# Gated values to DRAM, and a down projection by seven products of block sums behind the last block

## The chip, the core and the metric

One core of a Trainium2 chip runs one inference step of a one-layer decoder. The metric is the device time of that step in microseconds (us). The core has five engines that run beside each other and meet at semaphores: TensorE (PE, matmuls and weight loads), VectorE (DVE), ScalarE (ACT), GpSimd (POOL) and SyncE (SP), whose queue issues nearly all DMAs. The 16 DMA engines move the data that SP's queue names.

## The reference, cut to what matters

Everything is float32. Before the part that changes there are a combined input projection, dilated attention, a spatial gate and an output projection; they stay as they are. What changes is this part:

```python
def _swiglu(x, g, w_gate, w_up, w_down):
    h = _rmsnorm(x, g)
    return (jax.nn.silu(h @ w_gate) * (h @ w_up)) @ w_down
...
    x = x + jnp.concatenate([att, u * gate], axis=-1) @ w_out
    x = x + _swiglu(x, norm2_g, w_gate, w_up, w_down)
...
y_prompt = _rmsnorm(xp, final_g)
```

There are 2048 prompt tokens (16 tiles of 128 rows) and 32 sample tokens, 1024 model columns and 2816 hidden columns (22 slices of 128, called f below).

## The kernel before

Float32 matmuls are made of three passes each. An operand is split into a rounded high half (ACT copies it into the rounded type) and the rest, the low half (a subtraction on POOL or DVE), and a product is high by high, high by low, low by high.

The 16 token tiles go through the second half of the layer in three blocks: 6 tiles, 6 tiles, and 4 tiles with the sample rows. In each block the output projection and the second norm come first. Then a loop runs over the 22 slices f. In it the two products with `w_gate` and `w_up` are not made as eight block products but as seven (q = 0 to 6, function `product`): sums of blocks of the tokens and of the weights are multiplied, and the seven results are added up by DVE. Each of the seven is 12 matmuls whose moving side is 64 columns for each tile, 384 wide in a block of 6 tiles and 272 wide in the last one. The weight sums of a slice are made once, in the first block (`sums`, on POOL), are kept in DRAM (`ab_d`, 7 x 256 KB a slice) and are read back in the other two blocks (`load_source`). In the first block `gained` multiplies the raw weight quarters with the second norm's gain, kept in `g2c`, before sums are made of them. `high` and `low_half` split an operand into an `op` tile; `STAGES`, `prepare` and `ahead_of` say at which of the seven products of the slice ahead each of these steps stands.

`hidden` multiplies the gate with the up value and splits the result at once into the high and low half (`hw`). After every second slice, `down_unit` multiplies the two slices' halves with the split rows of `w_down` (`dw`, split on POOL) and DVE adds each 128 x 512 result to the tile's accumulator `acc` in SBUF (line 1763). So the down projection is plain: 16 tiles x 22 slices x 2 halves of the columns x 3 passes, 2112 matmuls of 512 columns, spread over the loops. Behind a block's last slice, `first_downs` and `down_unit` do the last pair, and `final_a`, `final_b` and `final_store` scale by the final norm and store `yp`. In the last block `last_rows` does this.

The order of the work is the order of the Python code; `later(n, fn)` puts a step n ticks ahead, and each product or unit calls `tick()`. All buffers come from pools with few copies: a step that needs a buffer waits until its last reader is done. SP's queue is in order, so that one DMA that waits holds up those behind it. The caches are copied from DRAM to DRAM in 128 pieces of 512 KB (112 whole ones of 512 KB and 16 of 504 KB), one at each `roll(1)`; `roll(len(pieces))` at the end issues what is left, which is nothing.

## Time and profile before

| what | value |
|---|---|
| median of 3 runs | 2527.84 us (2526.73 to 2529.05) |
| profiled execution | 2529.23 us, of which 2527.4 us is the span from the first to the last instruction |
| mean granted TensorE clock | 0.990 |
| PE, DVE, ACT, POOL busy | 2451.9, 1427.4, 1221.2, 1376.7 us |
| DMA | 480.00 MB moved, 190 GB/s on average |

The page gives for each engine its busy time. The share of a stage is read from a table of stretches (start:end in us), which gives for each engine the busy time, the granted clock, the mean share of the 16 DMA engines and the GB/s that they moved. In this execution the loops over f run from about 1030 to 1440 us (first block), 1600 to 2060 us (second) and 2165 to 2500 us (last).

### The profile page before, as it was taken

What the parts mean: (1) busy time and instruction counts of PE and PEld (TensorE: products, weight loads), DVE (VectorE), ACT (ScalarE), POOL (GpSimd) and SP (SyncE); (2) the same over time, 40 slices, a digit from 0 to 9 for tenths busy, and PEclk for the clock granted to TensorE, in tenths of its full rate; (3) what the DMA queues carried; (4) which work ended last, traced back from release to release, by engine and by line L of the source; (5) the groups of instructions that cost most, each with busy time, mean ns of one, the idle gap of its engine ahead of it and who ended that gap; (6) DMA issues with size and microseconds to landing.
All of it is one profiled execution on the core that took longest, in us unless ns stands there. A gap on an engine that the chain in (4) does not pass through costs nothing.

```text
span 2527.4 us, 38918 instructions
## 1 busy us (share of the span) xinstructions
PE 2451.9 (97%) x13598; PEld 2172.8 (86%) x13598; DVE 1427.4 (56%) x2768; ACT 1221.2 (48%) x2578; POOL 1376.7 (54%) x1078
## 2 busy tenths in 40 slices
PE   9999999999999899999999999999999999999997
PEld 7787777778888878999999988999999988999997
DVE  4378785347888866444444475444444466444445
ACT  6414344446877747545545446332323336444333
POOL 1245643233667657767767644653644534766664
PEclk9999999999999999999999999999999999999999
DMA  8863844887687674645646463663544643755553
GB/s 278 247 194 102 296 140 139 251 267 236 203 236 231 170 206 151 211 159 164 200 138 196 162 203 106 215 206 129 202 169 153 213 148 125 258 194 189 194 193 121
DMA packets 313585, 480.00 MB, mean 190 GB/s; under 512 B 25889, under 2 KB 178882, under 8 KB 307502
## 3 DMA queue, kind: packets, MB, share of 16 engines
q1 hardware_dynamic: 308428, 469.00, 57.6%
q10 hardware_dynamic: 4962, 8.51, 1.1%
q8 instruction: 108, 1.77, 0.3%
q14 instruction: 87, 0.71, 0.1%
HBM read 381.72 MB, written 165.83 MB: 217 GB/s over the span
## 4 chain that ended last, share of the span: by engine, by line
PE 57%; POOL 6%; issue 4%; DVE 4%; DMA 2%; ACT 2%; SPq 1%; DVEq 0%; ACTq 0%; POOLq 0%
PE ps_o L1761 18%; PE ps_m L1686 11%; PE ps_m L1684 11%; PE ps_m L1685 11%; POOL o L1108 1%; POOL ob L1110 1%; POOL ob L1106 1%; DMA pair<-f_d 1%; PE ps_o L1434 1%; PE ps_o L1433 1%; PE ps_o L1435 1%; DMA cat_d<-ob 1%; POOL qo L887 1%; DVE pl L944 1%; POOL op L1625 1%
## 5 line engine op out<-in xcount | busy, mean ns | idle before, releaser
L1625 POOL TENSOR_TENSOR op<-fr,op 128x512 fp32r<-128x512 f32 x393 | 499.3, 1300 | 279.4 <-ACT op L1621 267.5
L1686 PE MATMUL ps_m<-xh,op 128*128 128x384 f32 (+5 forms) x1932 | 610.2, 316 | 0.1
L1684 PE MATMUL ps_m<-xh,op 128*128 128x384 f32 (+5 forms) x1932 | 610.1, 316 | 0.0
L1685 PE MATMUL ps_m<-xl,op 128*128 128x384 f32 (+5 forms) x1932 | 609.1, 315 | 0.0
L1761 PE MATMUL ps_o<-dw,hw 128*128 128x512 f32 x2028 | 478.7, 391 | 3.7 <-DVE acc L1763 3.7
L1761 PEld LDWEIGHTS ps_o<-dw,hw 128*128 128x128 f32 x2028 | 377.9, 188 | 82.7 <-DVE acc L1763 7.0
L1763 DVE TENSOR_TENSOR acc<-acc,ps_o 128x512 f32<-128x512 f32 (+1 forms) x360 | 246.6, 687 | 220.4 <-PE ps_o L1761 220.4
L1684 PEld LDWEIGHTS ps_m<-xh,op 128*128 128x128 f32 x1932 | 363.8, 188 | 4.0
L1685 PEld LDWEIGHTS ps_m<-xl,op 128*128 128x128 f32 x1932 | 363.6, 188 | 3.5
L1686 PEld LDWEIGHTS ps_m<-xh,op 128*128 128x128 f32 x1932 | 363.5, 188 | 0.8 <-POOL op L1625 0.8
L1731 ACT ACTIVATE ps_t<-zn 128x384 f32<-128x384 f32 (+2 forms) x132 | 60.0, 454 | 457.1 <-DVE zn L1714 344.0
L1621 ACT ACTIVATE op<-fr 128x512 fp32r<-128x512 f32 x396 | 235.2, 623 | 20.1 <-DMA fr<-ab_d 17.2
L138 POOL TENSOR_TENSOR dw<-fd,dw 128x1024 fp32r<-128x1024 f32 x65 | 156.3, 2405 | 120.7 <-ACT dw L135 120.0
L323 PE MATMUL ps_s<-wh,xh 128*128 128x512 f32 x480 | 195.8, 408 | 6.1 <-ACT xh L135 6.0
L324 PE MATMUL ps_s<-wl,xh 128*128 128x512 f32 x480 | 190.7, 397 | 0.0
L325 PE MATMUL ps_s<-wh,xl 128*128 128x512 f32 x480 | 190.5, 397 | 0.0
L1741 ACT ACTIVATE hw<-ps_t 128x384 fp32r<-128x384 f32 (+2 forms) x132 | 57.7, 444 | 176.6 <-DVE ps_t L1737 175.6
L1625 POOL TENSOR_TENSOR op<-pair,op 128x512 fp32r<-128x512 f32 x63 | 81.2, 1295 | 98.8 <-ACT op L1621 94.6
L323 PEld LDWEIGHTS ps_s<-wh,xh 128*128 128x128 f32 x480 | 91.9, 191 | 35.1 <-issue 7.3
L325 PEld LDWEIGHTS ps_s<-wh,xl 128*128 128x128 f32 x480 | 91.7, 191 | 20.3 <-DVE xl L138 0.3
L324 PEld LDWEIGHTS ps_s<-wl,xh 128*128 128x128 f32 x480 | 92.0, 192 | 17.7 <-DVE wl L226 0.5
L1696 DVE TENSOR_TENSOR raw<-zn,ps_m 128x384 f32<-128x384 f32 (+1 forms) x63 | 32.5, 515 | 123.6 <-PE ps_m L1686 69.1
(503 smaller groups left out, 4801.4 us busy)
## 6 DMA issues: line engine op xcount, KB each, us to landing
fr<-ab_d SPq DMA_DIRECT2D x308, 256.0 KB
fd<-in_w_down_dram SPq DMA_DIRECT2D x66, 512.0 KB
out_ks_dram<-in_cache_k_dram SPq DMA_DIRECT2D x56, 512.0 KB
out_vs_dram<-in_cache_v_dram SPq DMA_DIRECT2D x56, 512.0 KB
ab_d<-fr SPq DMA_DIRECT2D x88, 256.0 KB
raw<-in_w_in_dram SPq DMA_DIRECT2D x72, 256.0 KB
qk_d<-pair SPq DMA_DIRECT2D x64, 256.0 KB
ab_d<-pair SPq DMA_DIRECT2D x63, 256.0 KB
```

The lines of the kernel that those rows point to most:

```text
L138: (eng_lo or pool).tensor_sub(lo, src, hi.bitcast(F32))
L323: pe.matmul(o[j], xh[:, k, :], wh, start=(k == 0), stop=False)
L324: pe.matmul(o[j], xh[:, k, :], wl, start=False, stop=False)
L325: pe.matmul(o[j], xl[:, k, :], wh, start=False, stop=(k == KD - 1))
L1621: act.activation(ops[f, j][0], ab[f][j], AF.Copy)
L1625: (pool if f or j else dve).tensor_sub(lo_, ab[f][j], hi.bitcast(F32))
L1684: pe.matmul(out, wh[:, ks], xh[:, :, k], start=(k == 0), stop=False)
L1685: pe.matmul(out, wh[:, ks], xl[:, :, k], start=False, stop=False)
L1686: pe.matmul(out, wl[:, ks], xh[:, :, k], start=False, stop=(k == 3))
L1731: act.activation(g, c, AF.Silu)
L1761: pe.matmul(ps[0:nr], l_, r_[:, cs], start=(z == 0 and y == 0), stop=(z == FC - 1 and y == len(pairs) - 1))
L1763: dve.tensor_add(B.acc[i][0:nr, cs], B.acc[i][0:nr, cs], ps[0:nr])
```

## The change

Slices 0 to 19 (ten pairs, `NJ = 10`) lose their down projection inside the loops. `hidden` writes the product unsplit into an `hr` tile, sorted into even and odd token tiles, and one DMA for each slice and block stores it to `h_d`. `x1_store` stores the rows after the output projection, with the last pair's share added (slices 20 and 21 are still projected as before), to `x1_d`, in the place where the final norm stood. The sample rows keep the old way.

Behind the last block `second_part` opens a pool `p2` over the loop's buffers and runs `Down`. It takes two halves of the tokens (hv, 1024 rows each, four pairs of an even and an odd tile), and in each seven products of block sums (s = 0 to 6), each a sum over the ten pairs j. So there are 140 steps n, of 12 matmuls of 512 columns each. The blocks are the even and the odd tiles (rows), the two slices of a pair (inner side) and the two halves of the columns of `w_down`. The sums run on DVE and POOL (`Down.sums`); those of `w_down` are made in the first half, stored to `t_d` and read again. The results of a product stay in four PSUM banks over ten steps and go to the accumulators in 4 additions (`evict`); some banks are added to twice and go on summing. Loads are issued six steps ahead, sums and splits three. 46 of the cache pieces are issued between the steps (n % 3 == 0); the loops issue 21 and 42.

The gain of the second norm is now multiplied into the token rows, in one DVE instruction with the norm's scale (`norm2_scale`), so `gained` and the tables for it are gone. `w_gate` and `w_up` come sorted by slice, so that a quarter is one contiguous load, and three of the seven sources are read from the input itself instead of a copy. In the first block sums move from POOL to DVE; in the last block the splits of `w_down` and two of the seven low halves do so.

```diff
-    EVEN_STAGES = ((), ((both_halves, 0), (keep, 3)), ...
+    STAGES = (((sums, 4), (sums, 3), (high, 0)), ((sums, 1), (keep, 4), (keep, 1), (low_half, 0), (high, 1)), ...
...
     def norm2_scale(B, i, r):
-        act.activation(B.xn[i][:n], B.acc[i][:n], AF.Copy, scale=r)
+        dve.scalar_tensor_tensor(B.xn[i][:n], B.acc[i][:n], r, gain[0][:n], op0=OP.mult, op1=OP.mult)
...
+                if fn is low_half and B.last and j in (1, 4):
+                    fn(f, j, dve)
...
+            if f < 2 * NJ and b == B.nt:
+                c0 = B.b0 * 64
+                sync.dma_start(h_d[f].rearrange("q p t -> p q t")[:, :, c0:c0 + B.nt * 64], B.h[f % FC][0])
...
+    def x1_store(B, i, nb):
+        t0 = (B.b0 + i) * P
+        sync.dma_start(x1_d[t0:t0 + P, :], B.acc[i])
...
+    EVICTS = ((0, 0), (0, 0), (0, 1), (1, 1), (1, 1), (0, 1), (1, 0))
+    NS = 7 * NJ
+    TAIL = 3
...
+        def fr(self):
+            return self.p2.tile([P, 512], F32, name="fr2", tag="fr2", bufs=10)
...
+        def load(self, n):
+            hv, s, j = self.at(n)
+            for key, y, q in (((("a11", 0, 0),), (("a21", 0, 1), ("a12", 1, 0)), (("a22", 1, 1),)) + ((),) * 4)[s]:
+                self.a[key, j] = t_ = self.p2.tile([P, 512], F32, name=key, tag=key, bufs=NJ)
+                sync.dma_start(t_, h_d[2 * j + y, q, :, hv * 512:(hv + 1) * 512])
+            if hv == 0 and s == 0:
+                w = [self.b(j, 0, 0), self.b(j, 0, 1), self.b(j, 1, 1, raw_tile)]
+            elif hv == 0 and s == 2:
+                w = [self.t(j, 2), self.b(j, 0, 0)]
...
+        def sums(self, n):
+            if hv == 0 and s == 0:
+                dve.tensor_sub(w[2], w[2], w[1])
+                dve.tensor_sub(w[1], w[1], w[0])
+                sync.dma_start(t_d[j, 2], w[2])
+                sync.dma_start(t_d[j, 0], w[1])
+            elif hv == 0 and s == 2:
+                pool.tensor_add(w[0], w[0], w[1])
+                sync.dma_start(t_d[j, 1], w[0])
...
+            elif s == 2:
+                self.src[n] = x = zn_tile()
+                dve.tensor_sub(x, a22, a21)
+                dve.tensor_add(a11, a11, x)
...
+        def split(self, n):
+            self.ops[n] = (hh, hl), (wh, wl) = op_tile(), op_tile()
+            h, w = self.src.pop(n), self.w.pop(n)[0]
+            act.activation(wh, w, AF.Copy)
+            act.activation(hh, h, AF.Copy)
+            pool.tensor_sub(wl, w, wh.bitcast(F32))
+            dve.tensor_sub(hl, h, hh.bitcast(F32))
...
+        def run(self):
+            for n in range(2 * NS - TAIL):
+                tick()
+                self.sums(n + 3)
+                self.split(n + 3)
+                self.load(n + 6)
...
+                if n % 3 == 0:
+                    roll(1)
+                self.mats(n)
+                if n >= NJ and j < 4:
+                    self.evict(phv, ps_, j, self.prev)
...
-            if f + 1 < NF and q in (1, 3, 5)[:(1, 3, 3 if f < 2 else 2)[bi]]:
+            if f + 1 < NF and q in (1, 4)[:(1, 2, 0)[bi]]:
                 roll(1)
...
         for n, u in enumerate(units):
             for q in range(7):
                 one(u, q)
-                if u["f"] % 2 == 0 and u["f"] > 0 and 3 <= q < 6:
-                    downs_of((B.h[0], B.h[1]), *((0, 2), (2, 4), (4, 9))[q - 3])
+                if B.last and u["f"] % 2 == 0 and u["f"] > 0 and q == 4:
+                    down_unit(B, len(rows) - 1, (B.h[0], B.h[1]))
```

On PE, in the second block between the products q = 3 and q = 4 of an even slice, before (`xh`, `xl` are the tokens' halves, `op` the weights', `dw` and `hw` the halves of `w_down` and of the gated values; x6 is six in a row):

```order
L1685 MATMUL ps_m_18920<-xl_15488,op 128x384
L1686 MATMUL ps_m_18920<-xh_15487,op 128x384
L1761 MATMUL ps_o_18941<-dw,hw 128x512 x6
L1761 MATMUL ps_o_18949<-dw,hw 128x512 x6
L1761 MATMUL ps_o_18957<-dw,hw 128x512 x6
L1761 MATMUL ps_o_18965<-dw,hw 128x512 x6
L1684 MATMUL ps_m_18973<-xh_15487,op 128x384
```

Twelve down matmuls for each of two tiles stood there. Now the next product follows at once:

```order
L1664 MATMUL ps_m_17071<-xh_13994,op 128x384
L1665 MATMUL ps_m_17071<-xl_13995,op 128x384
L1666 MATMUL ps_m_17071<-xh_13994,op 128x384
L1664 MATMUL ps_m_17092<-xh_13994,op 128x384
L1665 MATMUL ps_m_17092<-xl_13995,op 128x384
```

No down matmul stands between them. And on PE behind the last block, at the start of the new part:

```order
L1754 MATMUL ps_o_22591<-dw,hw 128x512 x6
L1754 MATMUL ps_o_22599<-dw,hw 128x512 x6
L1897 MATMUL ps_m_22628<-op 128x512
L1898 MATMUL ps_m_22628<-op 128x512
L1899 MATMUL ps_m_22628<-op 128x512
```

The down matmuls of 20 slices leave the loops and come back behind the last block as lines 1897 to 1899; over the whole program PE has 240 matmuls of 512 columns fewer (4688 for 4928) and the same number of every other width.

On SP, the head of the new part's loads (`a` is a block of `h_d`, `fr` and `raw` blocks of `w_down`, `t_d` the stored sums, `ac` and `x_d` the rows of `x1_d`):

```order
L1855 DMA t_d<-raw 128x512
L1856 DMA t_d<-fr_22587 128x512
L1834 DMA a_22686<-h_d 128x512
L1820 DMA fr_22688<-in_w_down_dram 128x512
L1820 DMA fr_22690<-in_w_down_dram 128x512
L1820 DMA raw<-in_w_down_dram 128x512
L1907 DMA ac<-x_d 128x1024 x2
L1782 DMA x_d<-acc_18410 128x1024
```

Stores of sums, loads of a later step and the traffic of the token rows share one queue, in this order; nothing of it stood there before. SP's end, before:

```order
L1330 DMA out_vs_dram<-in_cache_v_dram 16x8064
L1664 DMA fd<-in_w_down_dram 128x1024
L1808 DMA out_yp_dram<-acc_21019 128x1024
L1808 DMA out_yp_dram<-acc_21068 128x1024
L1808 DMA out_yp_dram<-acc_21121 128x1024
L1808 DMA out_yp_dram<-acc_21169 128x1024
L1810 DMA out_ys_dram<-acc_20969 32x1024
```

The last cache piece stood ahead of the last stores of rows. SP's end now:

```order
L1970 DMA out_yp_dram<-ac 128x512 x8
L1333 DMA out_vs_dram<-in_cache_v_dram 16x8192 x2
L1333 DMA out_vs_dram<-in_cache_v_dram 16x8064
L1333 DMA out_vs_dram<-in_cache_v_dram 16x8192 x7
L1333 DMA out_vs_dram<-in_cache_v_dram 16x8064
L1333 DMA out_vs_dram<-in_cache_v_dram 16x8192 x7
L1333 DMA out_vs_dram<-in_cache_v_dram 16x8064
```

Now 19 pieces of the caches (2 + 1 + 7 + 1 + 7 + 1) stand behind the very last store of rows.

On DVE, two steps of the first half's third product (hv 0, s = 2), a stretch that did not exist before:

```order
L1868 TENSOR_TENSOR zn<-a_23041,a_22751 128x512
L1869 TENSOR_TENSOR a_22453<-a_22453,zn 128x512
L1883 TENSOR_TENSOR op<-zn,op 128x512
L1868 TENSOR_TENSOR zn<-a_23066,a_22782 128x512
L1869 TENSOR_TENSOR a_22461<-a_22461,zn 128x512
L1883 TENSOR_TENSOR op<-zn,op 128x512
```

Three DVE instructions belong to a step. On POOL, the last step of the product ahead of it and two steps of this one:

```order
L1882 TENSOR_TENSOR op<-fr_23019,op 128x512
L1858 TENSOR_TENSOR fr_23043<-fr_23043,fr_23045 128x512
L1882 TENSOR_TENSOR op<-fr_23043,op 128x512
L1858 TENSOR_TENSOR fr_23068<-fr_23068,fr_23070 128x512
L1882 TENSOR_TENSOR op<-fr_23068,op 128x512
```

Each step there has three DVE and two POOL instructions whose operands all lie in SBUF; in the other products it has one to three on DVE and one on POOL.

More of the change, by code (lines that the diff above doesn't have):

```diff
@@ L1836, in last_rows, with second_part @@
+    def second_part(B, h):
+        m = len(B.rows) - 1
+        left.close()
+        gain.append(row_tile("final_g"))
+        d = Down(left.enter_context(tc.tile_pool(name="p2", bufs=1, reuse_waits="tile")))
+        for n in range(3):
+            d.load(n)
         first_downs(B, 0, 1, h)
-        squares(0, sa, 0)
-        squares(1, sa, 1)
+        d.sums(0)
+        d.split(0)
+        d.load(3)
         down_unit(B, m, h)
-        roots(sa, va, ra, 0, 2)
-        tick()
-        y = square_tile()
@@ L1856, in last_rows @@
-        squares(3, sb, 2)
-        scaled_row(2, rb_[:, 0:1])
-        roots(sb, vb, rb_, 2, 3)
-        newton(rb_[:, 2:3], vb[:, 2:3])
-        scaled_row(3, rb_[:, 2:3])
-        scaled_row(m, rb_[:, 1:2])
+        d.sums(1)
+        d.split(1)
+        d.load(4)
+        down_unit(B, 2, h)
+        d.sums(2)
+        d.split(2)
+        d.load(5)
+        down_unit(B, 3, h)
+        sync.dma_start(gain[1], dap(A["final_g"], 0, [[0, P], [1, D]]))
+        for i in range(m):
+            later(1 + i, x1_store, B, i, None)
@@ L1864, in hymba_step, with sample_final @@
+        def sample_final():
+            y = square_tile()
+            x = B.acc[m]
+            act.activation(y[0:SR], x[SR:2 * SR], AF.Copy)
+            dve.tensor_add(x[0:SR], x[0:SR], y[0:SR])
+            final_a(x[0:SR], O["ys"])
+        later(8, sample_final)
+        d.run()
     blocks = [Block(0, 6), Block(6, 12), Block(12, NT)]
@@ L2145, in hymba_step @@
             downs += [lambda B=B, pair=pair, i=i: down_unit(B, i, pair) for i in last[2:]]
-            finals = [lambda B=B, nb=nb, i=i: final_a(B, i, (load_acc, nb, i) if i < len(nb.rows) else None) for i in last]
+            finals = [lambda B=B, nb=nb, i=i: x1_store(B, i, nb) for i in last]
     roll(len(pieces))
     left.close()
+    stay.close()
     low.close()
```

311 lines of the change are left out of this document (186 added, 125 removed).

## The prediction

> **What bounds the kernel now.** I read the page first, then the table of stretches, then the chain of work that ended last.
>
> ```profile
> PE 2451.9 (97%) x13598; PEld 2172.8 (86%) x13598; DVE 1427.4 (56%) x2768; ACT 1221.2 (48%) x2578; POOL 1376.7 (54%) x1078
> ...
> 1020.00:1060.00 40.00, 38.84 (x201) 35.49 (x200) 16.69 (x28) 18.25 (x45) 29.37 (x23) 1.00 0.47 151
> 1060.00:1400.00 340.00, 340.00 (x1790) 318.12 (x1789) 150.56 (x254) 179.84 (x450) 246.43 (x183) 1.00 0.55 181
> 1440.00:1600.00 160.00, 158.72 (x855) 140.49 (x854) 95.44 (x213) 82.87 (x170) 83.78 (x62) 1.00 0.55 174
> 1600.00:2060.00 460.00, 460.00 (x2414) 429.54 (x2413) 204.93 (x345) 143.77 (x263) 226.22 (x162) 1.00 0.49 169
> 2060.00:2165.00 105.00, 101.16 (x587) 85.72 (x586) 70.59 (x168) 60.58 (x136) 50.33 (x37) 0.98 0.56 185
> 2165.00:2500.00 335.00, 335.00 (x2206) 308.62 (x2206) 161.63 (x353) 128.01 (x288) 216.00 (x156) 1.00 0.57 195
> 2500.00:2527.40 27.40, 14.31 (x68) 11.09 (x66) 19.77 (x41) 10.82 (x22) 4.79 (x2) 0.82 0.21 82
> ```
>
> In each row PE's busy time stands first, the granted clock, the DMA share and the GB/s last. In the three loops (1060, 1600, 2165) PE is busy all the time at the full clock, and the queue moves 169 to 195 GB/s: each matmul less is a gain there. Between the loops PE loses 1.2, 1.3 and 3.8 us (its time less its busy time), and behind the last slice 13.1.
>
> What a matmul costs is read from the chain, where a run of 24 down matmuls (two tiles) is one piece:
>
> ```profile
> 1032.94 5.48 PE ps_o L1761 x24
> 1040.53 5.48 PE ps_o L1761 x24
> ...
> 1086.17 5.48 PE ps_o L1761 x24
> 1116.64 5.48 PE ps_o L1761 x24
> ...
> 2168.02 5.49 PE ps_o L1761 x24
> ...
> 2201.96 5.49 PE ps_o L1761 x24
> ```
>
> From 1032.94 to 1040.53 lie 24 of them and one product of 12 matmuls, 384 wide: 7.59 us. From 1086.17 to 1116.64 lie 24 and twelve products: 30.47 us. The difference, 22.88 us, is eleven products, 2.08 us each; what is left is 5.51 us for 24, so 0.23 us for a matmul of 512 columns.
>
> **The change part by part.** *Fewer matmuls.* 2112 down matmuls less 192 that stay is 1920; the seven products take 140 x 12 = 1680. 240 x 0.23 = 55 us less on PE. A step n of the new part is 12 x 0.23 = 2.76 us of PE.
>
> *What feeds the new part.* In the loops nothing but the two operands had to arrive. Now all inputs come in by SP's queue in one stretch.
>
> ```profile
> 700.00:702.00 2.00, 2.00 (x21) 2.00 (x19) 1.97 (x5) 0.98 (x2) 2.00 (x3) 1.00 1.02 430
> 738.00:740.00 2.00, 2.00 (x20) 2.00 (x19) 2.00 (x5) 0.98 (x2) 2.00 (x2) 1.00 1.04 434
> ...
> 10.00:30.00 20.00, 20.00 (x85) 16.45 (x84) 12.82 (x16) 16.81 (x25) 8.67 (x6) 1.00 1.11 358
> ...
> 2524.42 0.33 SPq L1810 DMA_DIRECT2D out_ys_dram<-acc  x1
> ```
>
> The first three are stretches with all 16 DMA engines taken (share 1.0 and over): 434 GB/s in the best 2 us, 358 over 20 us in which the loads of transposed tokens come in 512-byte rows. The new part's rows are 2 KB and longer; I take 400, nearer the first rows, and keep 358 and 434 as ends. Up to the load for step 20 the queue carries, in blocks of 256 KB: ten steps with four loads and two stores (60), ten with three loads (30), step 20 (3), eight loads of token rows of two blocks (16), four `x1_store` (8), the gain (2), five cache pieces (10) and half a block: 129.5 blocks, 33.9 MB, 85 us at 400 GB/s (78 and 95 at the ends). It can start when PE has read the loop's last operand, and from there to step 0 PE has 24 + 8 + 12 + 12 = 56 matmuls, 12.9 us. A DMA's start and landing cost at most 2.3 us: the last row is the last issue before, done at 2524.75, 2.65 us ahead of the span's end at 2527.4, and its 128 KB need 0.3. Before PE can use it there are a POOL sum, an ACT copy and a POOL difference:
>
> ```profile
> L1625 POOL TENSOR_TENSOR op<-fr,op 128x512 fp32r<-128x512 f32 x393 | 499.3, 1300 | 279.4 <-ACT op L1621 267.5
> ...
> L1763 DVE TENSOR_TENSOR acc<-acc,ps_o 128x512 f32<-128x512 f32 (+1 forms) x360 | 246.6, 687 | 220.4 <-PE ps_o L1761 220.4
> ...
> L1621 ACT ACTIVATE op<-fr 128x512 fp32r<-128x512 f32 x396 | 235.2, 623 | 20.1 <-DMA fr<-ab_d 17.2
> ```
>
> 1.3 + 0.62 + 1.3 = 3.2 us. So step 20 is ready at 85 + 2.3 + 3.2 - 12.9 = 77.6 us after step 0 began, where PE could have it at 20 x 2.76 = 55.2: **22 us late** (15 to 32). By the Trainium skill ("DMA: Bandwidth & Descriptors", "Where 436 GB/s comes from"), transfers between HBM and SBUF are bound at about 358 GB/s a core, not by the fabric's 435; by that the queue would be 32 us late. The 430 and 434 above contradict it for 2 us each; no row here shows such a rate for longer.
>
> *The third product of the first half* (steps 20 to 29) has two POOL and three DVE instructions a step with all operands in SBUF. What such neighbours do to each other is seen at the start of the program:
>
> ```profile
> 8.43 1.42 DVE L226 SCALAR_TENSOR_TENSOR wl<-w,g1c,wh 128x512 fp32r<-128x512 f32 x2
> ...
> 13.40 5.24 DVE L226 SCALAR_TENSOR_TENSOR wl<-w,g1c,wh 128x512 fp32r<-128x512 f32 x3
> ...
> 13.39 4.70 POOL L138 TENSOR_TENSOR xl<-kv,xh 128x512 fp32r<-128x512 f32 x3 [1.07 <-ACT xh L135]
> ```
>
> Alone a DVE instruction takes 0.71 us and POOL's 1.3; three of each, started together, take 5.25 us, 1.75 a pair: they go one after the other but for some 0.25 us. So a step needs 2 x 1.75 and a third DVE instruction, 3.95 to 4.2 us, against PE's 2.76. I take 4.1: nine steps behind the first make **12 us**. If they did not hinder each other, POOL's own sequence sum, wait for ACT, difference would still need 3.2: 4 us; with full durations, 2 x 1.3 + 3 x 0.71 = 4.73: 18 us. The Trainium skill ("SBUF — State Buffer", "SBUF: two separate sides") says that VectorE and GpSimd have one port pair in common and that whoever holds it blocks the other for the whole instruction; by that sentence it is the 18, while the row has pairs at 1.75 and not at 2.0. Other products have one POOL and at most two DVE instructions (2.2 to 2.5 us, under 2.76) but for the second half's third (2.7 to 3.2 us): up to 4 us, covered by splits three steps ahead. From step 60 to 90 the queue has 124 blocks, 32.5 MB in 83 us, 392 GB/s; its lead of six steps, 16 us, hides small shortfalls. Together 1 us (0 to 8).
>
> DVE's additions into the accumulators read PSUM, and those rows do not suffer (line 1763 above has 687 ns on average beside a busy POOL, as short as 0.68 at the end, where POOL stands still), so `evict` costs nothing: PE is in another four banks for ten steps.
>
> *The end.*
>
> ```profile
> L1761 PE MATMUL ps_m<-dw,hw x12: 388/389/389, 2511.4 to 2513.9; 128*128 128x512 f32 x12
> ...
> 2516.09 0.68 DVE L1763 TENSOR_TENSOR acc<-acc,ps_m 128x512 f32<-128x512 f32 x1
> ...
> 2519.37 1.06 ACT L1821 ACTIVATE pair<-acc 128x1024 f32<-128x1024 f32 x1 [1.68 <-DVE acc L1763]
> ...
> 2520.55 0.15 DVE L1824 TENSOR_SCALAR s<-s 128x1 f32<-128x1 f32 x1
> ...
> 2521.92 2.47 DVE L1830 SCALAR_TENSOR_TENSOR acc<-acc,s,final_g 128x1024 f32<-128x1024 f32 x2
> ...
> 2514.40 9.17 SPq L1808 DMA_DIRECT2D out_yp_dram<-acc  x4
> ...
> L1330 SPq DMA_DIRECT2D out_ks_dram<-in_cache_k_dram x64: 515/516/608, 987.3 to 1876.4; - x64
> ```
>
> Before, the last matmul ends at 2514.3 and the span 13.1 us later; with 2.3 us for the landing and the closing in it. Now one addition (0.7), half a square (0.6), the root and its steps (2520.55 to 2521.92, 1.4, and 0.2 for one more), half a scaling (0.7) and two issues (0.7) lead to the last store, 4.3 us. Behind it SP issues 19 pieces (128 less 21, 42 and 46), 9.94 MB. Their issues (19 x 0.52) lie under the transfers: 24.9 us at 400 GB/s, 22.9 to 27.8 at the ends. 4.3 + 24.9 + 2.3 = 31.5 for 13.1: **18 us more** (16 to 21). Nothing hides it.
>
> *The loops without down matmuls.* A slice takes PE 7 x 2.08 = 14.6 us instead of 22.8 (5.51 x 3 / 2 more). POOL has seven low halves, 9.1 us, and the first block's sums on DVE add four instructions, about 1.8 to 2.8 us at the port: covered. In the last block two slices take 33.94 us (2168.02 to 2201.96, quoted above), of which 48 matmuls of 512 go: 22.9, so 11.5 us a slice. DVE has there seven additions (0.44 each), the products, two low halves (0.7 each) and the split of `w_down` (1.4), some 8 to 10 us with waits at the port, and it stands still while ACT waits for `w_down`:
>
> ```profile
> L1698 DVE TENSOR_TENSOR zn<-zn,ps_m 128x272 f32<-128x272 f32 x21 | 9.2, 439 | 20.3 <-PE ps_m L1686 20.3
> ...
> ACT dw L135 <- DMA fd<-in_w_down_dram: 64.2, 32, 3.5
> ```
>
> The last row is a wait: 32 times, 64.2 us in all, 2 us each, hidden before by 17 us slices. Four PSUM banks let PE run about 4.5 us ahead of DVE. I take 4 us (0 to 15). The `h_d` store (a DMA for each slice and block) makes SP wait for DVE at q = 6; the loads behind it have a slice of lead. The queue's load per slice, up to 3.7 MB in 14.6 us (252 GB/s), stays under 358.
>
> *Small edits.* `gained` goes (ACT), the weight loads become contiguous, the norm's gain moves from an ACT instruction to a DVE one of 1.3 us, while the finals between the blocks lose as much: PE's 1.2 and 1.3 us and part of the 3.8 go, -2 (-3 to 0).
>
> **The sum**: -55 + 22 + 12 + 1 + 18 + 4 - 2 = 0, with ends -22 and +43 if all fall together. It is made on a profiled execution of 2529.23 us (span 2527.4), 1.4 above the median; the difference is applied to the median, 2527.84. Of the unknown terms more can grow than shrink, so I set the forecast at +3: **2531 us**, no change (within 0.2%, 5 us, which is about what a measurement of this kernel can tell).
>
> **The rivals.** *Faster, 2511 us:* the new part's inputs hold PE little. The queue keeps its 434 GB/s (15 us late, tail 16) and the third product goes at POOL's own 3.2 us (4): -55 + 15 + 4 + 16 + 4 - 2 = -18. For it speak the two rows of 430 and 434 GB/s; against it the 5.25 us of the three pairs. It decides from where the new part's waits together stay under 30 us.
>
> *Slower, 2541 us:* the queue holds 358 GB/s over the 90 us, as the 20 us row has it: 32 + 12 + 1 + 21 + 4 - 2 - 55 = +13. Against it: that row has 512-byte packets in it. The section of the Trainium skill named above gives this result too.
>
> *Slower, 2548 us:* in the last block DVE, with the low halves and the `w_down` splits in its queue behind ACT's wait for `w_down`, keeps PE's banks: 0.9 us a slice make 20 instead of 4. Against it: 8 to 10 of 11.5 us is not full.
>
> *The change does not do what it says:* that the 240 matmuls do not go is excluded by PE's own list; that the 19 pieces end beside the last steps is excluded by SP's order.
>
> **How the numbers follow.** The forecast 0.36, the fast queue 0.29, the slow queue 0.18, the last block 0.17. The forecast's own range, 2522 to 2537, gives 0.02 faster, 0.27 same and 0.07 slower. Together faster 0.31, same 0.27, slower 0.42. The range to the rivals' centres and some way past them leaves out 2 in 10: 2510 to 2554; for the forecast alone 2522 to 2537.
>
> **What would show it.** Right: loops at 14.6 and about 11.5 us a slice with PE full; PE idle near the start of the new part, 22 us by step 20, with a DMA share of 1.0; steps 20 to 29 at 4.1 us with POOL and DVE busy in turn; 25 us of nothing but DMA at the end. Wrong: a PE that is full in the first thirty steps (then faster), gaps in the last block's loop, or a share of 1.0 at far fewer or more GB/s than 400.

## The result: slower by 3.65%

The changed kernel takes 2620.78 us (2616.99 to 2622.12, four runs) against 2528.1 (2526.73 to 2529.05, four runs): a ratio of 1.0365, 95% interval 1.0347 to 1.0383. The prediction was 2531 us, no change, with a range of 2510 to 2554 us: the measured time lies outside it. The profiled execution's span is 2615.2 us, 87.8 more than before.

### The profile after

The first line is the page's list of busy times. PE is no longer the engine that is always busy: its busy time is nearly that of before (2451.9 us), though it has 240 matmuls less, because in the new part a matmul counts for more busy time wherever PE is fed late. In the table below it is 79.47 us for 272 matmuls in the third row, at a granted clock of 0.86, and 34.33 us for 123 in the fourth, at 1.00, against 95.00 us for 421 in the sixth, where nothing waits.

```profile
PE 2447.1 (94%) x13358; PEld 2134.4 (82%) x13358; DVE 1641.3 (63%) x2866; ACT 1193.6 (46%) x2368; POOL 1305.2 (50%) x1036
```

The table of stretches, with columns as in the prediction: between the first two loops, the last block's loop, the new part up to step 20, its third product, steps 65 to 69, the steps from 100 on, and the end.

```profile
1310.70:1405.70 95.00, 90.47 (x403) 71.18 (x401) 56.51 (x105) 36.51 (x82) 36.94 (x28) 1.00 0.56 180
1840.00:2086.00 246.00, 236.75 (x1790) 227.62 (x1789) 155.50 (x345) 124.85 (x264) 133.25 (x101) 1.00 0.64 208
2090.70:2188.00 97.30, 79.47 (x272) 55.61 (x271) 55.67 (x80) 26.98 (x48) 26.31 (x19) 0.86 0.97 349
2193.00:2234.00 41.00, 34.33 (x123) 21.97 (x122) 40.34 (x35) 14.31 (x25) 34.27 (x21) 1.00 0.80 279
2333.00:2357.00 24.00, 18.20 (x58) 11.59 (x59) 18.31 (x30) 9.58 (x19) 8.38 (x7) 0.93 0.83 263
2453.00:2548.00 95.00, 95.00 (x421) 78.67 (x420) 73.52 (x77) 43.03 (x80) 55.35 (x39) 1.00 0.45 143
2580.00:2616.00 36.00, 0.00 (x0) 0.00 (x0) 0.00 (x0) 0.00 (x0) 0.00 (x0) 0.50 0.91 291
```

Of these rows only the sixth has PE full, as it was in all the loops before. In the third the DMA engines are (0.97, at 349 GB/s), in the fourth DVE and POOL are busy for 40.34 and 34.27 of 41 us, and in the last nothing runs but DMA, for 36 us.

The chain of work that ended last names the one that held each place (start, duration, what):

```profile
2011.81 3.77 DMA fd<-in_w_down_dram
...
2035.96 3.73 DMA fd<-in_w_down_dram
...
2098.38 5.80 DMA t_d<-raw
2104.24 3.13 DMA raw<-in_w_down_dram
...
2134.78 5.50 DMA fr<-in_w_down_dram
2140.34 6.96 DMA fr<-in_w_down_dram
...
2206.52 1.69 POOL fr L1858
2208.96 1.66 POOL op L1882
2210.62 1.70 POOL fr L1858
...
2333.09 1.34 DVE op L1883
2339.13 1.36 DVE op L1883
2345.18 1.35 DVE op L1883
...
2571.35 0.75 DVE ac L1967
...
2575.10 0.75 DVE ac L1967
```

It is read by its periods. In the last block a load of `w_down` returns every 24.15 us, a pair of slices. At the start of the new part all is DMA. In the third product two POOL instructions stand in each 4.1 us (2206.52 to 2210.62). In steps 65 to 69 a DVE instruction returns every 6.05 us. At the end DVE closes one tile every 3.75 us.

### Where the 88 us are

The starts of PE's matmuls in both traces give this account of the span. "Late" is against 12 matmuls in 2.72 us, the step that the trace shows wherever nothing waits.

| place | predicted | measured |
|---|---|---|
| 1920 matmuls of the loops (0.229 each) less 1680 (0.227) | -55 | -60 |
| norm phases and each block's first slice | -2 | +19 |
| slices of the first two blocks | 14.6 us | 14.56 us |
| last block, over what its matmuls need | +4 | +12 |
| last slice to step 0 | 0 | +3 |
| late at step 20 | +22 | +33 |
| steps 20 to 29, third product | +12 | +13.5 |
| steps 30 to 134 | +1 | +28 |
| steps 135 to 139 | 0 | +9.5 |
| last matmul to the end | +18 | +31 |

The measured ones sum to 89 of 87.8. In the second row, 3.4 us are the later start of the first loop, 983.1 us against 979.7; runs with the same code up to there start it between 977.7 and 986.5, so that may be scatter. The rest is found in every run with this code: 95.0 us from the first loop to the second instead of 88.5 (94.9 to 95.0 in those runs), 84.4 from the second to the third instead of 78.2 (84.3 to 87.5), and first slices 1.6, 0.6 and 1.0 us longer.

### The profile page after: what moved, and what is told of

Same layout as the page of the kernel before. It is cut to its first block, busy times and chain, and to the rows that moved or that the text cites. A ratio compares the mean times of both kernels' runs of the same rounds, so it can differ in the third digit from the quotient of the medians.

```text
span 2615.2 us, 39392 instructions
## 1 busy us (share of the span) xinstructions
PE 2447.1 (94%) x13358; PEld 2134.4 (82%) x13358; DVE 1641.3 (63%) x2866; ACT 1193.6 (46%) x2368; POOL 1305.2 (50%) x1036
## 3 DMA queue, kind: packets, MB, share of 16 engines
q8 instruction: 106, 1.74, 0.3%
## 5 line engine op out<-in xcount | busy, mean ns | idle before, releaser
L1621 POOL TENSOR_TENSOR op<-fr,op 128x512 fp32r<-128x512 f32 x352 | 463.5, 1335 | 295.7 <-ACT op L1617 277.2
L1664 PEld LDWEIGHTS ps_m<-xh,op 128*128 128x128 f32 x1932 | 363.9, 188 | 12.4 <-issue 11.2
L1882 POOL TENSOR_TENSOR op<-fr,op 128x512 fp32r<-128x512 f32 x140 | 202.5, 1452 | 250.8 <-ACT op L1880 244.3
L1617 ACT ACTIVATE op<-fr 128x512 fp32r<-128x512 f32 x396 | 230.8, 622 | 9.7 <-PE ps_m L1438 9.7
L1883 DVE TENSOR_TENSOR op<-a,op 128x512 fp32r<-128x512 f32 x120 | 151.2, 1268 | 72.2 <-ACT op L1881 72.0
L1880 ACT ACTIVATE op<-fr 128x512 fp32r<-128x512 f32 x140 | 88.3, 631 | 206.6 <-DMA fr<-in_w_down_dram 87.1
L1899 PE MATMUL ps_m<-op 128*128 128x512 f32 x280 | 115.6, 413 | 8.6 <-DVE op L1883 7.8
L1898 PE MATMUL ps_m<-op 128*128 128x512 f32 x280 | 115.0, 411 | 9.2 <-POOL op L1882 9.1
L1897 PE MATMUL ps_m<-op 128*128 128x512 f32 x280 | 114.5, 409 | 9.5 <-ACT op L1881 9.5
```

Source lines behind the costliest of these rows:

```text
L1617: act.activation(ops[f, j][0], ab[f][j], AF.Copy)
L1621: (eng or pool).tensor_sub(lo_, ab[f][j], hi.bitcast(F32))
L1664: pe.matmul(out, wh[:, ks], xh[:, :, k], start=(k == 0), stop=False)
L1882: pool.tensor_sub(wl, w, wh.bitcast(F32))
L1883: dve.tensor_sub(hl, h, hh.bitcast(F32))
L1897: pe.matmul(banks[m], hh[:, ts], wh, start=first, stop=False, skip_group_check=more)
```

## The experiments

A gain is given against the changed kernel, as the difference of the two ratios times 2525 us; each ratio has an interval of about 0.0017 to either side, so a gain is known to some 6 us (to 7 to 9 us in the combined runs at the end, whose intervals are up to twice as wide). What stands in the traces (a period, a lateness) is much sharper.

### The end: cache pieces

```diff
-            if f + 1 < NF and q in (1, 4)[:(1, 2, 0)[bi]]:
+            if f + 1 < NF and q in (1, 4)[:(2, 2, 0)[bi]]:
```

> Two cache pieces a slice in the first block's loop instead of one: 84 pieces go in the loops, 44 between the steps of the new part, none is left behind the last store. Theory (the end of the changed kernel is the 19 pieces alone: from 2580 to 2615 us the trace shows nothing but DMA): the time falls by 31 to 35 us, to 2586 to 2590 us, and the slices of the first block stay at 14.56 us. Rival (the pieces only move: the first block's loop, at 209 GB/s before, is held by them, or the new part's last steps are): the fall is under 20 us and the first block's slices are longer than 14.7 us.

Ratio 1.0227 (1.0212 to 1.0242), 35 us less; the first block's slices stay at 14.56 us. The end of SP's list of issues in this run:

```profile
2560.79 0.33 SPq L1349 DMA_DIRECT2D out_yp_dram<-ac  x1
2568.47 12.14 SPq L1970 DMA_DIRECT2D out_yp_dram<-ac  x8
```

Nothing follows the eight half rows, and the span ends at 2583.3. The whole end was the 19 pieces, and in the first block's loop they are free.

### The final norms inside the new part

First, what they cost in all:

```diff
-                    if ps_ == 5:
-                        self.final(phv * 8 + 2 * j)
-                    if ps_ == 6:
-                        self.final(phv * 8 + 2 * j + 1)
+                    if ps_ in (5, 6):
+                        i = phv * 8 + 2 * j + ps_ - 5
+                        sync.dma_start(O["yp"][i * P:(i + 1) * P, :], self.acc[i])
```

> Leaves out the final norm of the 12 tiles that are finished before the last product: their rows are stored as they are. Theory (steps 64 to 69 and 75 to 78 are held by a loop between DVE and ACT, in which the norm's root and its 1.29 us scaling stand ahead of the sum that ACT's next high half waits for: 6.05 and 5.4 us a step against 2.72): these steps come back to 2.7 to 3.3 us, and the time falls by 20 to 27 us, to 2594 to 2601 us. Rival (the same steps are held by the queue, by the t_d stores and loads and the yp stores): the steps stay over 4.5 us and the time falls by under 8 us.

Ratio 1.0253 (1.0237 to 1.0269), 28 us less. Steps 60 to 79 lose 4.6 us instead of 24.4, and steps 135 to 139 run at 2.72; 5.7 us appear in steps 80 to 84, so that 12.2 of the 28.4 us of steps 60 to 99 stay without any norm. The theory holds in the main: steps 75 to 78 come back to 2.72, but steps 65 to 67 only to 3.85, where 3.3 was the most expected. That the queue has no part is not shown by this run, since a store that waits for its norm waits less here too; in the changed kernel SP stands 11.5 us at three such stores between 2320 and 2400 us. How a norm holds a step is seen on DVE's timeline of the changed kernel (start, duration, instruction; in brackets the wait before it; the dots stand for four short steps of the root):

```profile
2339.13 1.34 DVE L1883 TENSOR_TENSOR op<-a,op 128x512 fp32r<-128x512 f32 x1 [1.30 <-ACT op L1881]
2340.40 0.68 DVE L1913 TENSOR_TENSOR ac<-ac,ps_o 128x512 f32<-128x512 f32 x1
...
2341.93 1.29 DVE L1796 SCALAR_TENSOR_TENSOR ac<-ac,s,final_g 128x1024 f32<-128x1024 f32 x1
2343.13 0.15 DVE L1457 TENSOR_SCALAR s<-s 128x1 f32<-128x1 f32 x1
2343.20 0.68 DVE L1861 TENSOR_TENSOR fr<-fr,fr 128x512 f32<-128x512 f32 x1
2345.18 1.35 DVE L1883 TENSOR_TENSOR op<-a,op 128x512 fp32r<-128x512 f32 x1 [1.30 <-ACT op L1881]
```

From low half to low half (1883) lie an addition (1913), the root's steps, the scaling (1796), the sum of `w_down` (1861), and then 1.30 us in which DVE waits for ACT, whose high half waits for that sum: 6.05 us where PE needs 2.72. Splits made three steps ahead cover 3 x 2.72 us of such losses, and from step 64 on PE is late.

Then the norms spread out, and the same with their steps in another place of the queues:

```diff
-                        self.final(phv * 8 + 2 * j)
+                        later(j if phv else 1 + 2 * j, self.final, phv * 8 + 2 * j)
-                        self.final(phv * 8 + 2 * j + 1)
+                        later(1 + 2 * j, self.final, phv * 8 + 2 * j + 1)
```

> On the changed kernel, the final norms are not begun in four steps in a row but one every third step (every second one in the second half); nothing is left out. Theory (DVE has 5.1 us of work a step where a final norm stands beside the sum, the split and an addition, and 3 on average): steps 60 to 79 lose 8 to 12 us instead of 25, the end is 3 to 8 us earlier, together 14 to 22 us less. Rival (what holds is that the loop DVE to ACT to DVE is in order, wherever the final norms stand): under 8 us.

Ratio 1.033 (1.0315 to 1.0345), 9 us less: between the theory's 14 to 22 and the rival's 8. Steps 60 to 79 lose 14 us instead of 24, but 80 to 89 lose 6 instead of 1, and a step with a norm is nearly as long as it was (5.99, 5.37). With the sum of `w_down` beside it there is little room.

```diff
-                tick()
                 self.sums(n + 3)
                 self.split(n + 3)
+                tick()
```

> On the changed kernel, the steps of the final norm that are due stand behind the split of a step instead of ahead of it, so that ACT's high halves no longer stand behind a root that waits for DVE. Theory (the two queues are tied together by that root): steps 64 to 69 and 75 to 78 fall from 6.05 and 5.4 us to under 5, the last steps too, together 10 us or more less, ratio under 1.0325. Rival (DVE has simply 5.1 us of work in such a step, and with its sum ahead of ACT's high half the order does not matter): under 5 us less.

Ratio 1.0361 (1.0341 to 1.0382): no change, and the long steps are 6.47 us. The theory of the tied queues fell here: with DVE's sum ahead of ACT's high half, the order gains nothing.

### The second norm's scale

```diff
-        dve.scalar_tensor_tensor(B.xn[i][:n], B.acc[i][:n], r, gain[0][:n], op0=OP.mult, op1=OP.mult)
+        act.activation(B.xn[i][:n], B.acc[i][:n], AF.Copy, scale=r)
```

> The second norm's scale is an ACT instruction again, and the gain is left out. Theory (DVE holds the transposes in the three norm phases, 3.4 + 6.5 + 6.2 us longer than before, because the 1.3 us scaling now stands in DVE's queue): these phases come back to within 2 us of those of before, and the time falls by 12 to 16 us, to 2605 to 2609 us. Rival (the phases are longer for other reasons: the x1 stores in SP's queue, the contiguous weight loads): under 5 us.

This kernel leaves the gain out, to price the instruction alone. Ratio 1.0271 (1.0256 to 1.0286), 24 us less, more than expected; its profiled span is 19.8 us shorter. The loops start at 975.7 us, lie 90.4 and 81.2 us apart, and the first slices are as short as before. 1.9 and 3.0 us of the two stretches stay, and what they come from was not looked into. PE's waits between the first two loops in the changed kernel (total us, times, longest):

```profile
PE ps_t L1499 <- DVE pair L1487: 3.7, 6, 1.6
PE ps_o L1754 <- DVE acc L1756: 1.1, 2, 0.6
```

The same stretch in this run:

```profile
PE ps_o L1754 <- DVE acc L1756: 1.1, 2, 0.6
PE ps_t L1499 <- ACT pair L1487: 0.2, 1, 0.2
```

The transposes (1499) waited for DVE's scaling (1487), once a tile, and no longer do. 1.3 us moved to an engine that was half idle (DVE is busy for 56.51 of 95.00 us between the first two loops) were not free, since the transposes behind them wait.

### The last block: `w_down`

```diff
+            pool_["fd2"] = fa.tile([P, D], F32, name="fd2", tag="acc5")
-        raws["d", f] = w_ = pool_["fd"]
+        raws["d", f] = w_ = pool_["fd2" if two_fd[0] and f % 2 else "fd"]
...
-                load_down(f + 1)
+                if B.last and f + 2 < NF:
+                    load_down(f + 2)
```

> A second buffer for the raw rows of w_down in the last block, so that each is loaded a whole slice before ACT copies it. Theory (once every two slices ACT waits 1.27 us for w_down, DVE waits 2.75 us for ACT, and PE waits 0.84 us for a bank that DVE has not read): the pair of slices goes from 24.15 us to 22.9 to 23.1 us, and the time falls by 11 to 14 us, to 2607 to 2610 us. Rival (DVE is full with its two low halves and the w_down splits and stays the bound): the pair stays over 23.8 us and the time falls by under 4 us.

Ratio 1.0326 (1.0308 to 1.0343), 10 us less, a little short: the pair is 23.77 us, not 22.9 to 23.1. The other half of the wait has another cause:

```diff
-                split_down(f, dve if B.last else None)
+                split_down(f)
```

> Like the run with two buffers for w_down, and the low halves of w_down go back to POOL in the last block. Theory (what is left of PE's wait, 0.58 us once in two slices, is DVE's low half of w_down that waits 1.74 us for ACT's high half): the pair goes from 23.77 to 23.1 to 23.3 us, 4 to 7 us less than with the two buffers alone. Rival (POOL, with 1.27 us for each low half and 2.5 for w_down, is late instead and the products wait for their operands): the pair at 23.7 us or more.

Ratio 1.0297 (1.028 to 1.0315), 17 us less; the pair is 23.09. The waits for `dw` in the changed kernel's last loop (total us, times, longest):

```profile
DVE dw L142 <- ACT dw L139: 47.7, 21, 3.8
...
ACT dw L139 <- DMA fd<-in_w_down_dram: 13.8, 10, 2.3
```

PE's waits there with two buffers:

```profile
PE ps_m L1668 <- DVE raw L1696: 4.0, 10, 0.4
```

And the loop with both edits, a row of the table of stretches:

```profile
1840.00:2070.00 230.00, 230.00 (x1755) 222.80 (x1755) 159.84 (x320) 123.09 (x260) 186.29 (x120) 1.00 0.69 223
```

In the changed kernel DVE stood still for 47.7 us in front of its low halves of `w_down`, because ACT's high halves were late, and ACT for 13.8 us because its load was. On POOL the low halves hold nobody that PE waits for, and PE is full.

### The queue up to step 20

```diff
-            later(1 + i, x1_store, B, i, None)
+            later(31 + i, x1_store, B, i, None)
...
-                if n % 3 == 0:
+                if n >= 30 and n % 7 in (0, 2, 4):
                     roll(1)
```

(The final gain and the four accumulators of the odd tiles go behind step 30 too.)

> On the changed kernel, of the 129.5 blocks of 256 KB up to step 20 28 are issued later (the four stores of x1, the final gain, four of the eight accumulators, ten cache pieces; 46 pieces still go between the steps and 19 behind the last store). Theory (the queue is short of bytes: 349 GB/s from 2090.7 to 2188 us): 7.3 MB less are 21 us, step 20 is 10 to 14 us late instead of 32, and the time falls by 18 to 23 us, to about 1.028 of the time before. Rival (not the bytes but the three raw tiles hold the queue: SP waits 9.9 us for the t_d stores from them): step 20 stays over 24 us late and the time falls by under 8 us.

Ratio 1.031 (1.0295 to 1.0326), 14 us less; step 20 is 16.8 us late instead of 32.7. In the runs with the queue as it was, step 20 is 29.3 to 36.2 us late, so the bytes count: some 16 us of the 21 expected. 5 us are given back in steps 55 to 69. Why, is not settled.

```diff
-                w = [self.b(j, 0, 0), self.b(j, 0, 1), self.b(j, 1, 1, raw_tile)]
+                w = [self.b(j, 0, 0), self.b(j, 0, 1), self.b(j, 1, 1, lambda: self.p2.tile([P, 512], F32, name="a22", tag="a22", bufs=NJ))]
```

> On the changed kernel, the third block of w_down of the first ten steps is loaded into the ten tiles that hold a22 later, instead of the three raw tiles, so that no load waits for a t_d store to leave its tile. Bytes and their order stay. Theory (the queue is short of bytes: the 16 DMA engines are 0.97 busy at 349 GB/s): step 20 stays 30 to 34 us late and the time is within 4 us. Rival (the raw tiles hold the queue, SP waits 9.9 us for them): step 20 8 us earlier or more, and 8 us less.

Ratio 1.033 (1.031 to 1.035), 9 us less; step 20 is 26.4 us late. Neither side is right alone: some six of the 33 us (3 to 10 against the other runs) were loads that waited for a raw tile. In its stretch up to step 20 the same bytes move faster:

```profile
2090.00:2183.00 93.00, 77.30 (x282) 55.21 (x281) 58.86 (x81) 28.10 (x50) 27.95 (x21) 0.93 1.00 375
```

Then the sums of `w_down` are taken out of the new part:

```diff
+            if bi == 1 and f < 2 * NJ:
+                down_sums(f, q)
...
+    def down_sums(f, q):
+        j, y = f // 2, f % 2
+        if q == 1:
+            if y == 0:
+                tw["x"] = [x.bitcast(F32) for x in ob_pair("tw")]
+            sync.dma_start(tw["x"][y], A["w_down"][f * P:(f + 1) * P, :])
+        if y and q >= 3:
...
+            (dve.tensor_add if v == 1 else dve.tensor_sub)(out, a, b)
+            later(2, sync.dma_start, t_d[j, v], out)
```

> On the changed kernel, the four block sums of w_down of each pair are made by DVE in the second block's loop from two loads and stored to t_d there; in the new part each step loads one block of w_down or t_d and makes no sum of w_down. Up to step 20 the queue then has about 88 blocks instead of 129.5. Theory (bytes and the VectorE-GpSimd port): step 20 is at most 5 us late instead of 32, steps 20 to 29 take 3.2 to 3.4 us instead of 4.1 (two low halves and two sums, 0.7 x 3 + 1.27), steps 64 to 69 under 5.5 us; the second block's slices stay at 14.56 us; together 38 to 46 us less, about 1.02 of the time before. Rival for the third product (POOL's own sequence of two instructions with the wait for ACT, not the port, sets the 4.1): steps 20 to 29 at 2.72. Rival for the loop: its slices over 14.8 us.

Ratio 1.0137 (1.0122 to 1.0152), 58 us less, more than expected. Step 20 is not late at all, steps 25 to 29 take 3.16 us, the second block's slices stay at 14.56, and steps 60 to 79 lose 13.2 us instead of 24.4, because DVE's sum is gone from them too. PE is full where it had stood:

```profile
2086.00:2182.00 96.00, 95.72 (x410) 74.93 (x410) 76.75 (x96) 40.48 (x73) 40.96 (x31) 1.00 0.94 355
```

The third product bears on the port that DVE and POOL have in common. With one POOL instruction and three of DVE a step takes 3.16 us; two of DVE at 0.68 and one of each that follow each other at the port, 0.7 and 1.27, are 3.3. DVE's and POOL's timelines of one step in this run show the wait:

```profile
2156.36 1.80 DVE L1865 TENSOR_TENSOR zn<-a,a 128x512 f32<-128x512 f32 x1
2158.20 0.69 DVE L1866 TENSOR_TENSOR a<-a,zn 128x512 f32<-128x512 f32 x1
2158.92 0.69 DVE L1880 TENSOR_TENSOR op<-zn,op 128x512 fp32r<-128x512 f32 x1
...
2156.32 1.29 POOL L1879 TENSOR_TENSOR op<-fr,op 128x512 fp32r<-128x512 f32 x1 [1.88 <-ACT op L1877]
```

The first DVE instruction starts beside POOL's and takes 1.80 us, the other two 0.69. With two instructions on POOL a step was 4.1 us: POOL's sum at 1.73, a wait of 0.75 for ACT, and its difference at 1.66. At the 1.29 us that POOL needs undisturbed, that sequence would still be 3.3. So the rival has its share, and the port adds some 0.8 us a step.

### All together, and what became late next

```diff
+            if B.rows[cur] == P:
+                B.xn[cur] = square_tile()
+                pool.tensor_mul(B.xn[cur], B.acc[cur], gain[0])
...
+            act.activation(B.xn[i], B.xn[i], AF.Copy, scale=r)
+            return
```

The four edits on rolls, sums, norms and `w_down`; the same with the lines above; and with only half of the columns that way:

> Four of the edits tried alone, together on the changed kernel: two cache pieces a slice in the first block, the sums of w_down made in the second block's loop, the final norms spread, two buffers for w_down with its low halves on POOL. Alone they gave 33, 57, 9 and 17 us. Theory (separate causes; and with no sum of w_down left on DVE in steps 60 to 69 the spread final norms cost nothing, where alone they still cost 6 us each): 119 to 126 us less than the changed kernel, ratio to the kernel before 0.986 to 0.990, steps 60 to 89 less than 4 us late in all. Rival (the causes overlap, PE's waits move to the next one): ratio over 1.0.

> The four edits together, and the second norm's gain multiplied in by POOL ahead of the root (128 x 1024), with the scale by the root on ACT, so that DVE has neither. Theory (DVE's queue held the transposes): the norm phases 5 to 8 us shorter each than in the run of the four edits, 15 to 22 us in all, ratio 0.978 to 0.984. Rival (POOL's product of some 2.6 us is later than the root, or holds DVE at the port): under 5 us gained, or a loss.

> As the run before in this list, but half and half: POOL multiplies the first 512 columns by the gain and ACT scales them, DVE does the other 512 in one instruction (0.7 us instead of 1.3). Theory: 10 to 20 us less than the four edits, within 5 us of the other version. Rival: as there.

Ratios 0.9928 (0.9912 to 0.9944), 0.9866 (0.9843 to 0.9889) and 0.9903 (0.9886 to 0.992): all three a little faster than the kernel before, and 110, 126 and 117 us faster than the changed one. The causes are separate, and nearly add up. 9 us are missing, which the intervals of four gains allow; the traces show six of them, since steps 60 to 79 are hardly late any more, but 80 to 99 are, by 10 us instead of 4. The gain on POOL gives 16 us (7 to either side), the halves 6. The phases did not each become 5 to 8 us shorter: with the gain on POOL the first loop begins 4.4 us earlier and the second follows after 90.8 us instead of 94.9, but the third after 85.9 instead of 84.6 (83.3 to 83.9 in the five runs below that keep the edit).

> The combined run with POOL's product (ratio 0.9866), with the final norm's steps behind the split. Theory of the tied queues: steps 80 to 92 and 137 to 139, 19 us late together, lose half of that; ratio 0.981 to 0.983. Rival (queue): steps 80 to 89 stay 8 us late or more, only the last steps change; ratio 0.984 or more.

> The combined run with POOL's product, with issues moved: accumulators of the second half loaded at steps 76 and 94 instead of 74 and 84, no cache pieces before step 26 and from 70 to 91, final norms two steps apart instead of three. Theory (queue): steps 80 to 92 lose under 4 us instead of 10, ratio 0.982 to 0.984. Rival (tied queues): steps 70 to 92 stay over 7 us late, ratio over 0.985.

```diff
-                if hv == 1 and s == 0 and j in (4, 5):
-                    self.acc_loads(1, 0, j - 4)
-                if hv == 1 and s == 1 and j in (4, 5):
+                if hv == 1 and s == 0 and j in (6, 7):
+                    self.acc_loads(1, 0, j - 6)
+                if hv == 1 and s == 2 and j in (4, 5):
...
-                if n % 3 == 0:
+                if n >= 26 and n % 2 == 0 and not 70 <= n < 92:
```

> Both of the last two, and the norms of the last four tiles overlapped (3.77 us each one after the other, against PE's 2.04 a tile). If both causes hold: no step but those of the third products is late (under 6 us in all), the end 4 us nearer to the last matmul, ratio 0.977 to 0.980.

0.9884 (0.9863 to 0.9905), 0.9852 (0.9819 to 0.9884), 0.9834 (0.9816 to 0.9852). Neither alone did what its theory said: 9 and 10 us stay in steps 65 to 90. Nor did both together: 9 us stay in steps 75 to 90. Without cache pieces ahead of step 26, though, the third product of the first half is hardly late (0 and 0.8 us): a step still takes DVE 3.17 us, but the splits are far enough ahead when it begins. What held steps 75 to 90 is in the last of the three, in SP's list of issues:

```profile
2281.33 0.33 SPq L1843 DMA_DIRECT2D fr<-in_w_down_dram  x1
2289.88 0.34 SPq L1349 DMA_DIRECT2D out_yp_dram<-ac  x1
2290.27 1.25 SPq L1857 DMA_DIRECT2D a<-h_d  x2
```

For 8.2 us, to 2289.88, SP issues nothing: the store of a finished tile stands in the queue, its norm is not done, and the loads behind it wait. Two runs issue these stores later, with the norm's steps behind the split and ahead of it:

```diff
-        later(1, sync.dma_start, out, x)
+        later(4, sync.dma_start, out, x)
```

> The last run (f3) with the stores of finished tiles issued four steps after the scaling instead of one. Theory (a store that waits for the final norm holds the loads behind it in SP's queue): no gap of more than 3 us in SP's issues from 2260 to 2310 us, steps 75 to 90 lose under 3 us instead of 9, ratio 0.979 to 0.982. Rival (the loads are late because too many bytes are asked for in these steps, 382 GB/s afterwards): they lose 7 us or more, ratio over 0.982.

> The same, but with the norm's steps ahead of the split as in the changed kernel. Theory (the order does not matter where DVE has no sum of w_down, as in the run that moved it alone): within 4 us of the other version. Rival: 5 us slower, in steps 60 to 80 and 137 to 139.

0.9821 (0.9801 to 0.9841) and 0.9849 (0.9828 to 0.987). In the first, SP's longest pause is 3.7 us instead of 8.2, and steps 75 to 90 lose 5.4 us instead of 9.2: more than the 3 expected, so the store was part of it and not all. All 135 steps together lose 6.0. In the second, steps 65 to 90 lose 11.2, so that without DVE's sum in the way the order shows in the steps. Step 138 takes 8.7 us instead of 4.9 there, but from the last matmul's start to the end it is 9.8 us instead of 13.6, which gives that back. The times do not decide: 0.9821 and 0.9849 lie 7 us apart, as much as their intervals allow by chance, and the combined run in which the order alone was changed was no faster (0.9884 for 0.9866). The first is the best version, 2481.36 us (2477.3 to 2486.5) against 2525.94:

```profile
PE 2395.1 (97%) x13358; PEld 2122.6 (86%) x13358; DVE 1612.1 (65%) x2838; ACT 1207.4 (49%) x2384; POOL 1381.1 (56%) x1064
```

PE's busy time is now 57 us below that of before, about the price of the 240 matmuls, which the changed kernel saved too and lost again in waits. How much the remaining edits would give the kernel before, without the seven products, was not tried.

## Why the prediction was wrong, point by point

*Right.* The matmuls (-55; -60, since in the new part one takes 0.227 us), the first two blocks' slices (14.6; 14.56) and the third product (12 at 4.1 us a step; 13.5 at 4.1). For the last, the Trainium skill ("SBUF — State Buffer", "SBUF: two separate sides") would have given 18, as an estimate; the trace has 13.5. Two POOL instructions at 1.29 us and three of DVE at 0.69 are 4.65 us, and a step takes 4.1, so they overlap a little.

*The queue, mis-sized.* 400 GB/s were taken, 349 came, and step 20 was 33 us late instead of 22. The rival with 358 GB/s had 32. The Trainium skill ("DMA: Bandwidth & Descriptors", "Where 436 GB/s comes from") gave that bound, and for a stretch this long the trace is near it; the 375 of the run without raw tiles and the 2 us at 434 in the trace of before are above it. The choice of 400 rested on rows of 2 us, though the one row of 20 us had 358. About 6 us of the 33 were not bytes but waits for the three raw tiles, which the prediction did not name.

*"Small edits, -2": the step that failed first.* The scaling was counted as 1.3 us that took the place of the finals' work. What counts is where it stands: DVE's queue, between the root and the transposes that PE waits for. These phases came out 19 us longer (3.4 of them perhaps scatter); the runs that took the scaling off DVE gained 16 and 24, each known to some 7.

*The last block, +4 (0 to 15): +12.* Within its ends, but the mechanism was that of a slower rival, DVE behind ACT behind the load of `w_down`, once a pair instead of once a slice.

*"Later stages, +1": the step that failed most.* The norms' work between the steps was not costed. The sum there counted POOL and DVE instructions of sums, splits and low halves, but not the 3 us that each of 12 final norms and its additions put on DVE in four steps in a row, in front of splits with a lead of three steps. 28 us were lost in steps 60 to 99 and 9.5 at the last steps. With the norms left out 12 and 0 remain, so some 26 us of the two belong to the norms. Most of what remains lies in steps 65 to 69 (4.5 us) and 80 to 84 (5.7). DVE's sum of `w_down`, in steps 60 to 69 too, has its part: with the norms kept and that sum gone the 28 us fall to 17. The cause of the 5.7 was not separated.

*The end, +18: +31.* The mechanism was right. Its size was not: the 19 pieces, issued from 2580.5, took 34.6 us and not 24.9 + 2.3, because the stretch moved 291 GB/s, nearly all of it copies from DRAM to DRAM, where 400 were taken; and the last four tiles close one after the other in 3.75 us each, so that the 4.3 us from the last matmul to the last store's issue were 9.

The gain was set too small by 5 us, and so was every loss, six of them by 8 us or more. Against one sure gain the sum of zero set losses of which four (the small edits, the queue, the later stages, the end) came out above the upper ends of their own ranges. Those ends add up to -23 and +39, not to the -22 and +43 that the prediction gives; 88 is beyond either.

## What to carry to other kernels

Work that is moved out of a balanced loop into a part of its own loses the cover that the loop gave: there count, step by step, every engine's work and every queue's bytes, final norms and stores included, against the bound engine's step, not the average. An instruction's price on a half idle engine is its place in that engine's queue, seen from whoever waits. And what need not be where it is (here cache copies, sums of weights, a gain) belongs in a loop with room, which turned 3.65% slower into 1.8% faster.

## What the runs showed of the hardware

The 16 DMA engines at shares of 0.97, 0.94 and 1.00 moved 349, 355 and 375 GB/s over more than 90 us, the first and the last with the same bytes in the same order. In the 36 us at the end, nearly all copies from DRAM to DRAM, it was 291 at 0.91. A DVE instruction of 128 x 512 with two operands in SBUF takes 0.69 us alone and 1.17 to 1.80 where a POOL one runs beside it; POOL's takes 1.29 alone and 1.66 to 1.74 in the third product. PE's granted clock was 0.86 from 2090.7 to 2188 us, where PE waited for data, and 1.00 in the same steps of the run that kept it fed. It was also 1.00 in the changed kernel's third product, where PE waits in every step. That the lower clock cost time of its own was not shown, since something else was late there.
